# A two-layer hybrid encoder on one Trainium2 core: v's second projection with its weights split early, merge products placed behind two heads, delta output by token tile

## The chip, the cores and the metric

The kernel runs on one core of one Trainium2 chip. The metric is device time in microseconds (us) of one execution, and the time of a kernel is the median over its runs. A core has five engines: TensorE (PE in the profile; PEld is its weight load), VectorE (DVE), ScalarE (ACT), GpSimd (POOL) and SyncE (SP, which here only issues DMAs). Each runs its own instructions in order, and they wait for one another with semaphores. SP, ACT and POOL each have queues of DMAs.

## The reference

x is 256 tokens by 1024. Two layers follow, and a final RMSNorm. A layer computes:

```
h = rmsnorm(x, norm_w[l])
proj = h @ w_in[l]                       # 1024 x 10272
(q_a, k_a, v_a, ab_a, z_a, q_b, k_b, v_b, z_b, gate_a, gate_b) = split(proj)
y_a = gated_delta_branch(q_a, k_a, v_a, ab_a, z_a, ...)        # 8 heads of 128, both directions
y_b = diff_attention_branch(q_b, k_b, v_b, z_b, cos, sin, ...) # 8 heads, two softmax maps each
x = x + (sigmoid(gate_a) * (y_a @ w_pa[l]) + sigmoid(gate_b) * (y_b @ w_pb[l])) @ w_out[l]
```

The delta branch runs a short convolution of five taps and a silu over q, k and v, and then the gated delta rule in chunks, forward and backward, for which a unit lower triangular matrix per head and chunk has to be inverted. Its output is normalised per head and multiplied with silu(z). The attention branch subtracts lambda times a second softmax map from the first, applies the result to v_b, normalises and multiplies with silu(z). All is float32.

## The kernel before

**Products.** A float32 weight is split into a high part that TensorE can take in one pass (`hi`, fp32r, a cast on ScalarE, L229) and the rest (`lo`, a subtraction on VectorE, L231). The activations are split likewise, and each product is three products: high by high, high by low, low by high. `weights` (L207) loads 512 columns of a weight in four parts of 256 rows (512 KB each, L225), splits each, and hands out eight k-tiles. By default the loads use the tag `raw` with three buffers, the parts `hi` and `lo` with two each. `homes` lets a part lie in a big tile that is free at that time (`A`, `ktm`, `vtm`, `B`), and `spare` puts a raw load into the tag `w4a`. `later` queues a part's cast and subtraction behind given instructions of ScalarE and VectorE, `held` moves a load to ScalarE's DMA queue behind the first normalisation.

**Three ways to multiply.** `proj_tm` (L236) accumulates both token tiles (of 128 tokens) together, k-tile by k-tile, in two of the four banks with tag `p`. `proj_by_tile` (L257) does one token tile through all eight k-tiles and then the other, each product queued behind the one before it. `proj_fm` (L285) gives channels by tokens and serves the convolutions: 96 products of 256 columns per half, and `evac_conv` (L511) reads the banks with four multiply-adds of VectorE per block of 128 channels (L521).

**Order.** The kernel's instructions are put in order by a planner, which works by program order, given priorities (`tc.high_priority`), data, buffers and a simulated time. `tc.issue_after(ins)` (in the helper `behind`) queues an instruction behind another on its own engine and adds no wait between engines. What runs when on the chip is thus not what the program's text alone says.

**A layer.** First v's first projection by token tile (columns C_VB to C_VB + 511, L366), in layer 0 while the tokens are still being loaded and normalised: `prenorm` (L327) normalises a token tile, transposes it on TensorE and splits it (L195, L196). Then, in the text's order (L877 to L905): k's convolution in two halves, v's second projection (`vb_part(1)`, through `proj_tm`), the decays, q's convolution, the projections of the attention's q and k, the weighted Gram matrices, the blockwise inversion on VectorE (`substitute`), v's convolution. The projection of beta and decay (`abp`, L480) comes ahead of k's convolution; its weights `wab` and `wabr` use the tags `raw` and `hi`. Eight `head`s follow (L823): scores (`sc`, L833), exponentials (L842), transposes (`at`, L853), a copy (L855), value products (`av`, L859). The projections of z lie between them.

**Merges.** `merges(g)` (L691) joins inverted blocks of 32 into blocks of 64 and then of 128, for two groups of four heads. A generator, it is advanced by `step`: loads; the first products (`y64p`, L717, queued behind `mark["av"]`); the second products (`zt64` at L731 and `z64` at L737, 64 and 32 of size 32 by 32) queued behind `mark["at"]`, the last transpose of the latest head; then the same for 128 (L754, L762). In the text both groups' second products come behind head 6 and ahead of head 7, with everything up to the chunks (`chunks`, L769) at high priority:

```
head(6)
with tc.high_priority(offset=HP):
    step(mg)
    step(mg)
    step(mg)
    in_step(chunks(0), chunks(1))
head(7)
```

**Output.** The attention's output goes through `gated` (L934), its gate and its projection; beside them the chunks finish. For the delta output, 16 squared sums (L976) of both token tiles are followed by one factor on GpSimd for both (`rsqrt_rows`, 16 columns, L136 and L137), then `gated`: 16 multiplications on VectorE (L939) with `split_T` (transposes `pt_ya` at L189, splits at L198 and L199) per half and token tile, and the projection `pa`. Its gate `ga` (L948) is projected at the same time.

**The start.** Token tile 0's loads, v's first two parts, token tile 1's loads and the taps `cwr` go on SP's queue, part 2 on ScalarE's behind the first normalisation's squares, part 3 on SP's when a raw buffer is free.

## Time and profile before

| | |
|---|---|
| median of 3 runs | 791.64 us (789.83 to 792.08) |
| the profiled execution | 792.5 us, its span 790.7 us |
| TensorE busy, weight load busy | 761.9 us (96%), 652.2 us (82%) |
| VectorE busy | 557.9 us (71%) |
| ScalarE busy | 479.2 us (61%) |
| GpSimd busy | 99.9 us (13%) |
| mean granted TensorE clock | 0.990 |
| DMA | 126.92 MB, 161 GB/s over the span |

The span reaches from the first to the last instruction of the profiled execution; the execution's own time is 1.8 us longer. Products are pipelined and their ends modelled, so a busy TensorE is not one at its peak; but idle time between rows is idle. In a row of the timeline stand the start, the time until the last of the group ended, engine, line, operation, the tiles written and read, shapes and count, and in brackets the engine's idle time before it and what ended it; "issue" there means that the profile shows nothing it waited for. The granted clock is 1.00 or 0.50 in any stretch.

### The profile page before, as it was taken

To read this page: it belongs to the slowest core of one execution; us is meant where nothing else is said; L and a number is where in the kernel's file an instruction comes from. 1 tells how busy PE (TensorE), PEld (TensorE's weight loads), DVE (VectorE), ACT (ScalarE), POOL (GpSimd) and SP (SyncE) were. 2 spreads that over 40 slices of the span, in tenths; PEclk is the share of its full clock that TensorE was granted. 3 is DMA by queue.
4 is the path that set the end of the run, shared out by engine and by line. 5 is a ranking of instruction groups with operands and counts; after the bars stand their busy time and mean duration, and the time that the engine had idled before them with its cause. 6 is when DMAs were issued, how large, how long until landed. Compare 5 with 4: busy or idle time off the path is not lost.

```text
span 790.7 us, 13805 instructions
## 1 busy us (share of the span) xinstructions
PE 761.9 (96%) x5222; PEld 652.2 (82%) x5222; DVE 557.9 (71%) x1047; ACT 479.2 (61%) x1043; POOL 99.9 (13%) x133
## 2 busy tenths in 40 slices
PE   7989999999998999999999899999999899999996
PEld 4989889887787888878889788899778688887884
DVE  4587968999973653477656977989998445546772
ACT  4557776556676745664534778655577675446551
POOL 4200471100030100100000025510001110001000
PEclk9999999999999999999999999999999899999998
DMA  6555657564395534357625557655446925344631
GB/s 195 153 181 159 204 170 202 162 173 145 110 204 177 187 109 132 107 161 239 219 80 165 156 165 236 186 167 162 140 139 190 205 85 183 124 123 125 218 129 53
DMA packets 77746, 126.92 MB, mean 161 GB/s; under 512 B 19679, under 2 KB 20015, under 8 KB 77680
## 3 DMA queue, kind: packets, MB, share of 16 engines
q1 hardware_dynamic: 73182, 115.22, 48.7%
q0 software_dynamic: 3936, 9.77, 4.9%
q8 instruction: 41, 0.67, 0.4%
q10 hardware_dynamic: 562, 1.05, 0.4%
q14 instruction: 25, 0.20, 0.1%
HBM read 121.27 MB, written 4.75 MB: 159 GB/s over the span
## 4 chain that ended last, share of the span: by engine, by line
PE 80%; DVE 9%; ACT 4%; DMA 4%; issue 2%; POOL 0%; SPq 0%; POOLq 0%; ACTq 0%; DVEq 0%
PE pp_vb L280 3%; DMA raw_q<-in_w_in_dram 3%; PE pp_qk L244 2%; PE sc L833 2%; PE pp_qk L245 2%; PE pp_qk L243 2%; PE av L859 2%; PE pp_o L280 2%; PE pf_v L295 2%; PE pp_gb L243 2%; PE pp_za L244 2%; PE pf_v L299 2%; PE pf_v L297 2%; PE pp_gb L245 2%; PE pp_gb L244 2%
## 5 line engine op out<-in xcount | busy, mean ns | idle before, releaser
L244 PE MATMUL pp_qk<-lo_qk,hT 128*128 128x512 f32 x128 | 51.3, 401 | 1.0 <-DVE lo_qk L231 1.0
L245 PE MATMUL pp_qk<-hi_qk,hT 128*128 128x512 f32 x128 | 50.1, 391 | 0.0
L243 PE MATMUL pp_qk<-hi_qk,hT 128*128 128x512 f32 x128 | 46.1, 398 | 0.7 <-ACT hi_qk L229 0.7
L231 DVE TENSOR_TENSOR lo_qk<-raw_qk,hi_qk 128x1024 fp32r<-128x1024 f32 x32 | 40.2, 1256 | 9.0 <-ACT hi_qk L229 8.7
L229 ACT CAST hi_qk<-raw_qk 128x1024 fp32r<-128x1024 f32 x32 | 33.5, 1046 | 20.1 <-PE pp_qk L245 12.6
L231 DVE TENSOR_TENSOR lo_pb<-raw_pb,hi_pb 128x1024 fp32r<-128x1024 f32 x16 | 19.6, 1224 | 34.2 <-ACT hi_pb L229 34.2
L295 PE MATMUL pf_q<-hT,hi_q 128*128 128x256 f32 x128 | 36.3, 288 | 0.2 <-ACT hi_q L229 0.2
L295 PE MATMUL pf_v<-hT,hi_v 128*128 128x256 f32 x128 | 36.5, 289 | 0.0
L297 PE MATMUL pf_v<-hT,hi_v 128*128 128x256 f32 x128 | 36.2, 285 | 0.0
L297 PE MATMUL pf_q<-hT,hi_q 128*128 128x256 f32 x128 | 35.8, 284 | 0.0
L295 PE MATMUL pf_k<-hT,hi_k 128*128 128x256 f32 x128 | 35.7, 283 | 0.0
L297 PE MATMUL pf_k<-hT,hi_k 128*128 128x256 f32 x128 | 35.6, 283 | 0.0
L842 ACT ACTIVATE es<-sc,mx 128x256 f32<-128x256 f32 x64 | 29.7, 472 | 9.6 <-DVE mx L840 9.5
L299 PE MATMUL pf_q<-hT,lo_q 128*128 128x256 f32 x128 | 35.2, 290 | 0.0
L231 DVE TENSOR_TENSOR lo_gb<-raw_gb,hi_gb 128x1024 fp32r<-128x1024 f32 x16 | 19.6, 1222 | 21.9 <-ACT hi_gb L229 21.9
L299 PE MATMUL pf_v<-hT,lo_v 128*128 128x256 f32 x128 | 34.6, 285 | 0.0
L299 PE MATMUL pf_k<-hT,lo_k 128*128 128x256 f32 x128 | 34.3, 286 | 0.0
L231 DVE TENSOR_TENSOR lo_k<-raw_k,hi_k 128x1024 fp32r<-128x1024 f32 x16 | 19.6, 1223 | 16.2 <-ACT hi_k L229 16.2
L521 DVE SCALAR_TENSOR_TENSOR cvk<-pf_k,cw,cvk 128x254 f32<-128x254 f32 (+1 forms) x64 | 29.3, 478 | 2.0 <-ACT cvk L517 1.2
L521 DVE SCALAR_TENSOR_TENSOR cvv<-pf_v,cw,cvv 128x254 f32<-128x254 f32 (+1 forms) x64 | 29.7, 475 | 0.6 <-ACT cvv L517 0.5
L521 DVE SCALAR_TENSOR_TENSOR cvq<-pf_q,cw,cvq 128x254 f32<-128x254 f32 (+1 forms) x64 | 29.6, 475 | 0.7
L231 DVE TENSOR_TENSOR lo_ga<-raw_ga,hi_ga 128x1024 fp32r<-128x1024 f32 x16 | 19.4, 1223 | 15.0 <-ACT hi_ga L229 15.0
(361 smaller groups left out, 2508.3 us busy)
## 6 DMA issues: line engine op xcount, KB each, us to landing
raw_qk<-in_w_in_dram SPq DMA_DIRECT2D x32, 512.0 KB, 3.7
raw_k<-in_w_in_dram SPq DMA_DIRECT2D x16, 512.0 KB, 3.7
raw_q<-in_w_in_dram SPq DMA_DIRECT2D x16, 512.0 KB, 3.7
raw_v<-in_w_in_dram SPq DMA_DIRECT2D x16, 512.0 KB, 3.8
raw_zb<-in_w_in_dram SPq DMA_DIRECT2D x16, 512.0 KB, 3.6
raw_za<-in_w_in_dram SPq DMA_DIRECT2D x16, 512.0 KB, 3.7
raw_gb<-in_w_in_dram SPq DMA_DIRECT2D x16, 512.0 KB, 4.3
raw_o<-in_w_out_dram SPq DMA_DIRECT2D x16, 512.0 KB, 4.5
```

What stands on the lines that cost most here:

```text
L229: high = S.copy(hi[:, :, :n], raw[:, :, :n]).ins
L231: mark[nm, kp] = high, V.tensor_tensor(lo[:, :, :n], raw[:, :, :n], hi[:, :, :n].bitcast(F32), ALU.subtract).ins
L243: T.matmul(o, act[kt // 4][:, 0, kt % 4, ts_], hi, start=kt == 0, stop=False)
L244: T.matmul(o, act[kt // 4][:, 0, kt % 4, ts_], lo, start=False, stop=False)
L245: mark["proj"] = T.matmul(o, act[kt // 4][:, 1, kt % 4, ts_], hi, start=False, stop=kt == KT - 1).ins
L280: mark["proj"] = T.matmul(o, a_, w_, start=kt == 0 and a_ is ah and w_ is hi, stop=kt == KT - 1 and a_ is al).ins
L295: T.matmul(o, hi[:, cs], act[kt // 4][:, 0, kt % 4, :], start=first, stop=False, skip_group_check=True)
L297: T.matmul(o, hi[:, cs], act[kt // 4][:, 1, kt % 4, :], start=False, stop=False, skip_group_check=True)
L299: T.matmul(o, lo[:, cs], act[kt // 4][:, 0, kt % 4, :], start=False, stop=done, skip_group_check=True)
L521: V.scalar_tensor_tensor(ca[:, o0:o1], acc[:, b, o0 + sft : o1 + sft], cw[:, j, cb : cb + 1], ca[:, o0:o1], ALU.mult, ALU.add)
L833: mm = T.matmul(sp[n][:, qt * SEQ : (qt + 1) * SEQ], qkT[h // 4][rows, 0, h % 4, qt * P : (qt + 1) * P], qkT[h // 4][rows, 1, h % 4, :], s ...
L842: S.activation(es[:, n, qt, :], spv[:, qt, :], AF.Exp, bias=mx[:, n, qt : qt + 1], accum_out=s_all[:, h, n, qt : qt + 1])
```

## The change

- *v's second projection* goes by token tile through `proj_by_tile` instead of `proj_tm`. Its four parts get homes of their own: a pair with tag `p8`, the second half of the tile `B` (now twice as long) and `vtm`. Its raw loads use `w4a`. Parts 0 and 1 are split behind the split of token tile 1's second half, parts 2 and 3 behind the second and third part of k's first half. In layer 0 the loads of parts 0 and 1 go on ScalarE's queue, behind that split.
- *Loads one by one*, in layer 0's start: part 1 of v's first projection on ScalarE's queue behind token tile 0's first squares, token tile 1's loads behind its second squares, part 2 behind the cast of part 0; `wab` behind the cast of part 2.
- *Smaller moves*: `wab` and `wabr` use the tags `w2a` and `w2c`; sine and cosine are one activation; the lambda sums (`lp`, `lq`, `ls`, `neglam`) move behind the gates of beta and decay.
- *Merges*: group 0's second products stay behind head 6, group 1's come behind head 7, each queued behind that head's last value product and no longer behind its last transpose.
- *Delta output*: squares, factor and `gated` for token tile 0, and then for token tile 1.

```
-                with behind(mark["norm", 0][0] if kp in held else None):
-                    (nc.scalar if kp in held else nc.sync).dma_start(
+                load = (held or {}).get(kp)
+                with behind(load):
+                    (nc.scalar if load else nc.sync).dma_start(
...
-    def tokens(m):
+    def tokens(m, load=None):
         for i in range(2):
-            nc.sync.dma_start(out=xt[i][:, m, :], in_=xdr[:, i, m, :])
+            with behind(load):
+                (nc.scalar if load else nc.sync).dma_start(out=xt[i][:, m, :], in_=xdr[:, i, m, :])
...
-        places = list(homes((("A", 1), ("ktm", 1), ("vtm", 1), ("B", 1)), f"vb{l}"))
-        later, between = {}, None
+        places = list(homes((("A", 1), ("ktm", 1), ("vtm", 1), ("B", 2)), f"vb{l}"))
+
+        places2 = pair(f"wvb{l}")
+        places2 = [t_.rearrange("p x b t -> p x (b t)").rearrange("p x (k c) -> p x k c", k=2)
+                   for t_ in places2] + [places.pop(), *homes((("vtm", 1),), f"vb{l}1")]
+        later, between, held = {}, None, {}
         if l == 0:
             later[0] = None, mark["norm", 0][1]
             def between(kt):
                 if kt == 2:
+                    held[1] = mark["square", 0, 0]
                     later[1] = mark["split", 0, 0]
                 elif kt == 4:
-                    tokens(1)
+                    tokens(1, mark["square", 0, 1])
+                    held[2] = mark["vb00", 0][0]
...
-        wab = wpool.tile([P, 2, 512], F32, tag="raw", name=f"wab{l}", bufs=3)
...
+        wab = work.tile([P, KT, 32], F32, tag="w2a", name=f"wab{l}", bufs=2)
+        with behind(None if l else mark["vb00", 2][0]):
+            (nc.sync if l else nc.scalar).dma_start(
+                out=wab, in_=wl[:, C_AB : C_AB + 32].rearrange("(k p) c -> p k c", p=P))
+        wabr = work.tile([P, KT, 64], F32R, tag="w2c", name=f"wabr{l}", bufs=3)
...
-            first = mark["at"]
+            first = mark["av"]
...
         conv("k", C_KA, 0, 0)
         conv("k", C_KA, 0, 1)
-        vb_part(1)
+        for _ in proj_by_tile(hT, wl, C_VB + 512, evac_v(1), f"vb{l}1", places2, spare=range(4),
+                              later={0: mark["split", 1, 1], 1: mark["split", 1, 1],
+                                     2: mark[f"k{l}0", 1], 3: mark[f"k{l}0", 2]},
+                              held={} if l else dict.fromkeys(range(2), mark["split", 1, 1][0])):
+            pass
         log_decays()
...
         head(6)
         with tc.high_priority(offset=HP):
-            step(mg)
+            step(mg[:1])
+        head(7)
+        with tc.high_priority(offset=HP):
+            step(mg[1:])
             step(mg)
             step(mg)
             in_step(chunks(0), chunks(1))
-        head(7)
...
-        def gated(o_, z_, r_, nw_, yT, nm):
+        def gated(o_, z_, r_, nw_, yT, nm, tiles=range(NM)):
             for i in range(2):
-                for m in range(NM):
+                for m in tiles:
...
+        ro = small.tile([P, NM, NH], F32, tag="ro", name=f"ro{l}")
+        yaT = pair(f"yaT{l}")
         for m in range(NM):
             for h in range(NH):
                 S.activation(sqj[:, :P], osb(h // 4, m)[:, h % 4, :], AF.Square,
                              accum_out=sso[:, m, h : h + 1])
-        V.tensor_tensor(sso, sso, rq2, ALU.mult)
-        ro = small.tile([P, NM, NH], F32, tag="ro", name=f"ro{l}")
-        rsqrt_rows(ro.rearrange("p c h -> p (c h)"), sso.rearrange("p c h -> p (c h)"), 1.0 / P, 16)
-        V.scalar_tensor_tensor(ro, ro, 0.5, rq, ALU.mult, ALU.mult)
-        yaT = pair(f"yaT{l}")
-        gated(osb, za, ro, nw[:, 0:1], yaT, f"ya{l}")
+            V.tensor_tensor(sso[:, m], sso[:, m], rq2[:, m], ALU.mult)
+            rsqrt_rows(ro[:, m], sso[:, m], 1.0 / P, NH)
+            V.scalar_tensor_tensor(ro[:, m], ro[:, m], 0.5, rq[:, m], ALU.mult, ALU.mult)
+            gated(osb, za, ro, nw[:, 0:1], yaT, f"ya{l}", (m,))
         branch(yaT, w_pa[l], gta, f"pa{l}")
```

54 lines of the change are left out of this document (23 added, 31 removed).

## The prediction

> **What bounds the kernel now.** I read the page first, then the list of what TensorE waited for, then busy time by stage, then single stretches of the timeline.
>
> ```profile
> span 790.7 us, 13805 instructions
> PE 761.9 (96%) x5222; PEld 652.2 (82%) x5222; DVE 557.9 (71%) x1047; ACT 479.2 (61%) x1043; POOL 99.9 (13%) x133
> ...
> PE pp_vb L243 <- DVE cvk L521: 3.1, 2, 1.5
> PE pp_ga L244 <- DVE lo_ga L231: 2.1, 2, 1.0
> PE pp_vb L244 <- DVE lo_vb L231: 1.0, 2, 0.5
> ```
>
> TensorE is the bound: it stands idle for 790.7 - 761.9 = 28.8 us in all, and no edit of this change takes a matrix product away. So a gain can only be idle time of TensorE, or time in which its clock was granted at half. The three waits shown each come twice, once per layer; the first and the third are v's second projection, the second is the gate beside the delta output. The next view gives TensorE's busy time in four stretches (columns: the stretch, its length, busy time and count of PE, PEld, DVE, ACT, POOL, then the granted clock, the DMA share and GB/s).
>
> ```profile
> 28.40:50.50 22.10, 22.10 (x184) 21.89 (x183) 13.97 (x24) 13.18 (x19) 0.00 (x0) 1.00 0.53 150
> 50.50:75.00 24.50, 22.35 (x139) 19.34 (x138) 20.36 (x37) 18.39 (x49) 0.00 (x0) 1.00 0.52 153
> 435.00:460.00 25.00, 22.88 (x143) 19.86 (x143) 21.24 (x37) 17.93 (x48) 0.00 (x0) 1.00 0.54 163
> 331.00:350.00 19.00, 17.95 (x87) 14.63 (x86) 12.68 (x28) 10.27 (x19) 3.11 (x2) 1.00 0.47 144
> ```
>
> Idle is length less PE busy: 2.15 and 2.12 us around v's second projection, 1.05 us at the delta output of layer 0 (that of layer 1 has the other half of the wait for lo_ga), none in k's convolution ahead of the projection. The fourth place is the merge, once per layer, in the same columns:
>
> ```profile
> 242.86:246.27 3.41, 1.38 (x24) 0.89 (x17) 1.83 (x2) 3.31 (x9) 0.00 (x0) 1.00 0.62 187
> 246.27:249.68 3.41, 3.41 (x50) 2.54 (x53) 1.44 (x6) 2.41 (x10) 0.00 (x0) 0.50 0.81 297
> 625.15:628.56 3.41, 0.95 (x37) 0.68 (x36) 1.23 (x1) 1.54 (x3) 0.00 (x0) 1.00 0.31 114
> 628.56:631.97 3.41, 3.24 (x72) 2.40 (x71) 0.00 (x0) 2.24 (x6) 0.00 (x0) 0.50 0.91 300
> 631.97:635.39 3.42, 3.42 (x96) 3.14 (x96) 2.02 (x6) 2.51 (x11) 0.00 (x0) 0.50 0.03 13
> ```
>
> A stretch in which TensorE is busy for 1.38 (or 0.95) of 3.41 us is followed by one (or two) at half the clock. The idle time is 2.03 and 2.46 us here; the half clock costs half of 3.41 us in layer 0 and half of 3.24 + 3.42 us in layer 1, so 1.7 and 3.3 us. All that the merge could give is 2.03 + 2.46 + 1.7 + 3.3 = 9.5 us.
>
> **v's second projection.** Rows of the timeline (start, length) show the largest wait and the spare time ahead of it, and one of the chain what 24 products of this form take:
>
> ```profile
> 58.24 0.47 PE L243 MATMUL pp_vb<-hi_vb,hT 128*128 128x512 f32 x1 [1.54 <-DVE cvk L521]
> ...
> 38.10 1.05 ACT L229 CAST hi_k<-raw_k 128x1024 fp32r<-128x1024 f32 x1 [1.83 <-PE pf_k L297]
> ...
> 39.18 1.23 DVE L231 TENSOR_TENSOR lo_k<-raw_k,hi_k 128x1024 fp32r<-128x1024 f32 x1 [1.66 <-ACT hi_k L229]
> ...
> 386.78 5.45 PE pp_o L280 x24
> ```
>
> The 1.54 us are a bank: this product is the first into the accumulator of the other token tile, and VectorE had not read k's first convolution out of it. Four lo parts of v, 4 x 1.23 = 4.9 us, stand on VectorE among those reads. The change makes them earlier, in buffers that the convolution's weights don't use, and runs all 24 products of token tile 0 before the first of tile 1. Like the 24 of the row from the output projection they take 5.45 us in the first bank, longer than the 1.54 us wait, and VectorE comes sooner as well. Both waits go: 2.15 + 2.12 = 4.27 us. What it adds ahead: four times 1.05 us of ScalarE and 1.23 us of VectorE per layer, beside k's weights. These have gaps of 1.83 and 1.66 us per pair of k-tiles, each of which holds one part; the cover is thin, and where it fails a k product waits up to 1.05 or 1.23 us. I take 4.0 (ends 4.3 and 0). What is late next is VectorE, 20.36 of 24.50 us busy in that stage, but it loses 4.9 us there.
>
> In layer 0 two of the four loads are issued by ScalarE's queue behind the splits of token tile 1, two instructions; what is queued behind them there is k's first cast, not needed before the convolution. The weights of beta and decay leave the convolution's raw and hi buffers, and lambda's sums move behind them; sine and cosine become one activation. All of this lies off TensorE's waits: nothing.
>
> **The start.** Part 0 of v's weights comes late, and part 3 shows what a load takes by itself:
>
> ```profile
> 1.71 8.09 DMA raw_vb<-in_w_in_dram
> ...
> 11.40 7.76 PE pp_vb L280 x19
> ...
> 12.15 0.40 SPq L225 DMA_DIRECT2D raw_vb<-in_w_in_dram  x1
> ...
> 15.63 1.04 ACT L229 CAST wB_vb<-raw_vb 128x1024 fp32r<-128x1024 f32 x1 [0.18 <-DMA raw_vb<-in_w_in_dram]
> ```
>
> 8.1 us against 15.63 - 12.15 = 3.5. With the loads one by one, part 0 could land up to 4.6 us sooner. But the loads that are held back stand behind part 0 on SP's queue already, so it need not gain from their going; and part 2 is now issued only when part 0 has been cast (after 9.8 at today's landing, and 3.5 us later it is there, at 13.3, where tile 1's normalisation waits for its lo part). I take nothing, with ends of 2 us gained (less than half of the 4.6, as tile 1 needs the later loads too) and 1.5 us lost (part 0 sharing with the loads that now come from another queue).
>
> **The merge.** TensorE's rows, layer 1 first, with ScalarE's copy of head 6's weights, and then the like of layer 0:
>
> ```profile
> 623.28 1.33 PE L717 MATMUL y64p<-T,A 32*32 32x32 f32 x128
> ...
> 625.64 0.45 PE L731 MATMUL zt<-U__96,y 32*32 32x32 f32 x32
> 628.73 0.49 PE L731 MATMUL zt<-U__96,y 32*32 32x32 f32 x21 [2.64 <-issue]
> ...
> 630.02 2.08 PE L833 MATMUL sc<-qkT 64*128 64x256 f32 x8
> ...
> 626.27 0.58 ACT L855 COPY aT<-at 128x512 f32<-128x512 f32 x1
> ...
> q8 instruction: 1, 0.02, 3.0%
> ...
> 246.21 0.98 PE L833 MATMUL sc<-qkT 64*128 64x256 f32 x2 [2.03 <-issue]
> ...
> 241.88 0.72 PE L731 MATMUL zt<-U__96,y 32*32 32x32 f32 x62
> ...
> 243.41 0.58 ACT L855 COPY aT<-at 128x512 f32<-128x512 f32 x1
> ...
> 249.12 0.94 PE L731 MATMUL zt<-U__96,y 32*32 32x32 f32 x64
> ...
> 251.91 0.76 ACT L747 ACTIVATE T<-z 32x256 f32<-32x256 f32 x2
> ...
> 255.03 2.08 PE L754 MATMUL y128p<-T,A 64*64 64x64 f32 x64
> 257.04 1.16 PE L859 MATMUL av<-vb,aT 128*128 128x128 f32 x8
> ```
>
> In layer 1 TensorE stops for 2.64 us in the middle of a run of equal products that wait for nothing. The row of queue 8 is from DMA traffic at 626 to 628 us: one block of instructions was fetched there, during the stop. I read the stop as TensorE having run out of instructions, since 128 + 96 small products (each with a weight load) go by in about 3 us. The change lets 8 score products and head 6's 8 value products go first. Layer 1: scores follow at 625.64 and take half of 2.08, to 626.7; the copy is done at 626.85; the value products take about 1 us, to 627.9; of the 32 products that were left before the stop, 16 remain, 0.2 us; if the block comes at 628.73 as before, the stop is 0.6 + 0.15 in place of 2.64, a gain of 1.9. The stretch 625.15 to 628.56 is then busy for about 2.6 us and not 0.95, so the clock should hold: 3.3 more. After the second products TensorE may run dry until head 7's exponentials free their banks, about 1 us: 4.0 taken. Layer 0: scores from 241.88 to 242.9, copy done at 243.99, value products to 244.9, second products to 246, block at 246.21: about 1.2 us idle for 2.03, a gain of 0.8; the stretch is busy for about 2.2 of 3.41 us, and whether that holds the clock I count at half of 1.7, less 0.6 dry: 1.0. Together 5.0 (ends 9.5 gained and 2 lost, the latter if the stop and the half clock stay and 1 us of dry time comes in each layer).
>
> **Delta output.** VectorE runs all 16 products of the gated output in a row, ahead of a weight part:
>
> ```profile
> 337.93 4.29 DVE L939 SCALAR_TENSOR_TENSOR kq<-kq,ro,za 128x128 f32<-128x128 f32 x16
> ...
> 343.41 0.50 PE L244 MATMUL pp_ga<-lo_ga,hT 128*128 128x512 f32 x1 [1.05 <-DVE lo_ga L231]
> ...
> 334.07 2.90 POOL L137 TENSOR_TENSOR ro<-rspre,mhalf 128x16 f32<-128x16 f32 x1
> ...
> 344.41 1.40 DVE L199 SCALAR_TENSOR_TENSOR yaT<-pt_ya,nw,yaT 128x512 fp32r<-128x512 f32 x2
> ...
> 348.54 1.03 PE L189 MATMUL pt_ya<-ident,kq 128*128 128x128 f32 x8
> ```
>
> By token tile they come in two runs of 8, 2.15 us each, and GpSimd's power of 2.90 us becomes two of about half. One weight part can slip between, which is worth 1.05 us per layer. Added are one multiply, one GpSimd pair and one scaling per layer, small and beside other work. I take 1.4 of 2.10 (ends 2.1 gained, 1 lost if both runs fall ahead of a weight part).
>
> **Sum.** 4.0 + 0 + 5.0 + 1.4 = 10.4. The profiled execution took 792.5 us (span 790.7, 1.8 around it), so 782.1; the median of the runs is 791.64, 0.86 below it, so 781.2.
>
> **Rivals.** *The stop follows the products*: what counts is that small products come in a burst, wherever it stands, so the idle time and half clock stay or move to group 1's burst. For it: the "issue" rows don't say what was missing. Against: the stop is in the middle of one burst. The merge gives nothing and 5.4 is left of the sum, 786.2. [...] Chance 0.15.
>
> *The clock stays at half*: what holds the clock is not busy time as the view counts it, and small products and scores on half the rows don't count. For it: the stretch 628.56 to 631.97 was busy for 3.24 us and one more at 0.50 followed. Against: 242.86 to 246.27 and 625.15 to 628.56 are the idlest of the stage, and both times the half clock came right behind. The merge then gives idle time alone, 1.9 + 0.8 less the dry 1.6, so 1.1, and the median is 791.64 - 6.5 = 785.1. [...] Chance 0.15.
>
> *Early parts collide*: the gaps of 1.83 and 1.66 us are missed and each part costs k's convolution 0.5 us, 2 x 4 x 0.5 = 4.0 us, v's whole gain: 785.2. For it: the gaps are only 0.8 and 0.4 us longer than a part. Against: ScalarE and VectorE are busy for 13 and 14 of 22.1 us there. Chance 0.08.
>
> *The delta chain ends late*, which ends slower: group 1's second products ran at 249.12, head 7's value products at 257.04 + 1.16. If these keep their place, group 1 starts 9.1 us later. Its next step ran at 255.03, 2.4 us after its last input (251.91 + 0.76), so the chain of merges and chunks is 6.7 us late. The chain's last transposes ran at 348.54, 2.7 us after the banks were read (344.41 + 1.40): that is the slack. 4.0 us per layer are left, and where the chain sets the end the idle time saved beside it is no gain: 8.0 - 4.0 of v = 4.0 lost, 795.6. It decides if head 7's value products come over 2.4 + 2.7 us after 249.12. Against: scores of head 7 go first now, and without the stop its exponentials come sooner. Chance 0.08.
>
> *More than I take*: clock held in both layers and the start 2 us sooner, 10.4 + 2 + 2.5 = 14.9: 776.7. Chance 0.12. *The forecast*: 0.42, from 778 to 785.
>
> **Numbers.** 781.2 us. The range goes from 775.5 to 789.5: it holds the forecast, the three rivals that take one term away and most of the case with more, and leaves out the late chain and the ends of all unknowns together. This kernel's measurement tells 0.3% from no change, 2.4 us: faster is below 789.3. Forecast, the three one-term rivals and the case with more give 0.92 if each stood alone; of that I count 0.1 for two terms failing together, 0.09 of it within 0.3% and 0.01 slower, which joins the late chain's 0.08. Faster 0.82, same 0.09, slower 0.09.
>
> **What would show it.** Right: no wait of pp_vb for cvk or lo_vb, and TensorE busy throughout 50 to 65; no "issue" stop above 1 us at zt and no half-clock stretch in layer 1; L939 in runs of 8 and no wait of pp_ga for lo_ga; first product of v within 1.5 us of 11.4. Wrong: pf_k waiting for hi_k or lo_k in k's convolution; a stop of 2 us in front of group 1's products; pp_pa waiting for yaT.

## The result and the profile after

| | before | after |
|---|---|---|
| median | 791.86 us (789.83 to 795.11, 4 runs) | 781.91 us (780.45 to 784.95, 4 runs) |
| the profiled execution | 792.5 us, span 790.7 us | 782.13 us, span 780.3 us |

The ratio is 0.9888, 95% interval 0.9856 to 0.992: about 10 us less, and the prediction said 781.2. The total came out nearly as worked out. Its terms did not, and most of what follows is about that.

First the head of the page of the changed kernel.

```profile
span 780.3 us, 13801 instructions
...
PE 758.2 (97%) x5222; PEld 651.5 (83%) x5222; DVE 557.0 (71%) x1051; ACT 474.9 (61%) x1042; POOL 101.0 (13%) x137
```

The count of products is the same, and TensorE's idle time is 780.3 - 758.2 = 22.1 us where it was 28.8. That is 6.7 us of the 10.4 by which the span is shorter; the rest is busy time that became shorter, through the clock above all (mean granted 0.994 after 0.990; 0.004 of 780 us are 3.1 of the 3.7). Next, three lines of the list of what TensorE waited for (total, times, longest).

```profile
PE abq L480 <- ACT abT L477: 2.8, 1, 2.8
...
PE zt L735 <- issue: 1.1, 1, 1.1
...
PE pf_k L296 <- ACT vb L348: 1.0, 1, 1.0
```

The three waits that the prediction quoted (pp_vb for cvk, pp_ga for lo_ga, pp_vb for lo_vb) are gone. In their place stand two waits for ScalarE, each once and both early in layer 0, and what is left of the stop among the merge's small products. Busy time in the stages that were shown of before (columns as there):

```profile
28.00:50.50 22.50, 19.68 (x139) 19.41 (x138) 13.12 (x27) 13.23 (x19) 0.00 (x0) 0.85 0.48 140
50.50:72.00 21.50, 21.50 (x139) 19.39 (x138) 17.54 (x37) 11.83 (x35) 0.00 (x0) 1.00 0.36 108
...
432.00:455.00 23.00, 23.00 (x151) 20.90 (x151) 16.88 (x33) 13.92 (x45) 0.00 (x0) 1.00 0.30 87
...
325.00:346.50 21.50, 21.50 (x126) 18.74 (x125) 13.57 (x30) 13.19 (x42) 3.67 (x4) 1.00 0.38 120
```

In v's second projection of both layers (second and third row) and at the delta output (fourth) TensorE now has no idle time at all. The first row is new trouble: 22.50 - 19.68 = 2.8 us idle in k's convolution of layer 0, at a mean clock of 0.85, where before it was busy throughout at 1.00.

How far each stage moved is read from where the same work begins. Rows of TensorE, of the kernel before and then of the changed one: the first product of v in layer 1, and the first product of q's convolution, which follows v's second projection, in both layers (v's first product in layer 0 was at 11.40 before).

```profile
67.54 0.36 PE L295 MATMUL pf_q<-hT,hi_q 128*128 128x256 f32 x1
...
398.33 0.71 PE L280 MATMUL pp_vb<-wA_vb,hT 128*128 128x512 f32 x2
...
451.56 0.36 PE L295 MATMUL pf_q<-hT,hi_q 128*128 128x256 f32 x1
```

```profile
9.03 3.45 PE L281 MATMUL pp_vb<-wA_vb,hT 128*128 128x512 f32 x6
...
69.00 0.28 PE L296 MATMUL pf_q<-hT,hi_q 128*128 128x256 f32 x1
...
395.80 1.55 PE L281 MATMUL pp_vb<-wA_vb,hT 128*128 128x512 f32 x4
...
445.87 0.28 PE L296 MATMUL pf_q<-hT,hi_q 128*128 128x256 f32 x1
```

From v's first product to q's convolution layer 1 took 53.23 us and takes 50.07: 3.2 gained. Layer 0 took 56.14 and takes 59.97: 3.8 lost. The start is 2.4 us earlier, and at 69.00 all of it is gone, with 1.5 more. Why is seen in ScalarE's rows of the changed kernel:

```profile
24.69 1.05 ACT L230 CAST wvb<-raw_vb 128x1024 fp32r<-128x1024 f32 x1 [3.92 <-DMA raw_vb<-in_w_in_dram]
28.54 1.05 ACT L230 CAST wvb<-raw_vb 128x1024 fp32r<-128x1024 f32 x1 [2.80 <-DMA raw_vb<-in_w_in_dram]
...
33.26 0.35 ACT L477 COPY abT<-abp 64x256 f32<-64x256 f32 x1
```

These are the early parts 0 and 1. Their loads were issued at 17.39 and 18.49 us and landed at 24.7 and 28.5, after 7.3 and 10.0 us; v's part 3 of the kernel before took 3.5. ScalarE stands at both casts, for 3.92 and 2.80 us, and runs nothing else in that time. Behind them come a copy of v, two table loads (1.28 us each) and the copy `abT`, for which TensorE waits:

```profile
33.66 1.06 PE L480 MATMUL abq<-id,abT 64*128 64x32 f32 x4 [2.82 <-ACT abT L477]
```

```profile
20.00:28.00 8.00, 7.29 (x41) 6.28 (x42) 4.24 (x12) 1.82 (x4) 1.34 (x3) 1.00 0.99 325
28.00:33.52 5.52, 2.84 (x24) 2.63 (x22) 2.15 (x7) 4.71 (x8) 0.00 (x0) 1.00 0.67 191
33.52:40.35 6.83, 6.69 (x30) 6.63 (x31) 4.45 (x11) 3.70 (x5) 0.00 (x0) 0.50 0.33 100
```

The second fence gives busy time again. In its second row TensorE is idle for 2.7 of 5.52 us, and then 6.83 us at half the clock. These hold 30 products, the next 6.83 us, at the full clock, hold 58, most of them of the same form; so the half clock is put at half of 6.69, another 3.3, here and likewise below. Layer 0's own waits in v's second projection are gone all the same (2.15 us before, none now); what it lost, it lost ahead of them.

The merge of layer 1, TensorE's rows and the stretch around the stop:

```profile
622.42 0.32 PE L735 MATMUL zt<-U__96,y 32*32 32x32 f32 x15
623.86 0.59 PE L735 MATMUL zt<-U__96,y 32*32 32x32 f32 x47 [1.11 <-issue]
```

```profile
620.62:624.03 3.41, 2.18 (x49) 1.54 (x49) 2.59 (x4) 2.00 (x8) 0.00 (x0) 1.00 0.37 74
624.03:627.44 3.41, 2.83 (x91) 2.39 (x82) 1.14 (x4) 3.30 (x14) 0.00 (x0) 1.00 0.78 288
```

The stop is 1.11 us and no longer 2.64, after 15 products (before: after 32), and the clock stays at 1.00. In layer 0 there is no stop there. But group 1's products of layer 0 are late:

```profile
241.32 1.33 PE L721 MATMUL y64p<-T,A 32*32 32x32 f32 x128
...
257.27 1.05 PE L863 MATMUL av<-vb,aT 128*128 128x128 f32 x8
258.26 0.72 PE L735 MATMUL zt<-U__96,y 32*32 32x32 f32 x62
...
261.91 2.08 PE L758 MATMUL y128p<-T,A 64*64 64x64 f32 x64
```

They ran at 249.12 before, and the next step at 255.03. Measured from the merge's first products (239.52 before, 241.32 after) that step comes 15.5 us later before and 20.6 after: the delta chain is 5.1 us late. And the delta output, on VectorE:

```profile
336.09 2.18 DVE L949 SCALAR_TENSOR_TENSOR kq<-kq,ro,za 128x128 f32<-128x128 f32 x8
...
343.47 2.18 DVE L949 SCALAR_TENSOR_TENSOR kq<-kq,ro,za 128x128 f32<-128x128 f32 x8
```

Two runs of 8, with the weight parts between them.

### The profile page after: what moved, and what is told of

Its sections match the earlier page's. It is cut to its first block, busy times and chain, and to the rows that moved or that the text cites. A ratio compares the mean times of both kernels' runs of the same rounds, so it can differ in the third digit from the quotient of the medians.

```text
span 780.3 us, 13801 instructions
## 1 busy us (share of the span) xinstructions
PE 758.2 (97%) x5222; PEld 651.5 (83%) x5222; DVE 557.0 (71%) x1051; ACT 474.9 (61%) x1042; POOL 101.0 (13%) x137
## 4 chain that ended last, share of the span: by engine, by line
PE 81%; DVE 7%; DMA 6%; ACT 4%; issue 1%; POOL 0%; SPq 0%; POOLq 0%; ACTq 0%; DVEq 0%
PE pp_vb L281 4%; DMA raw_q<-in_w_in_dram 3%; DMA raw_vb<-in_w_in_dram 3%; PE pp_qk L245 2%; PE pp_qk L246 2%; PE pp_qk L244 2%; PE pp_o L281 2%; PE pf_v L296 2%; PE pf_k L300 2%; PE pf_k L296 2%; PE pf_k L298 2%; PE pp_za L245 2%; PE pf_v L300 2%; PE pf_v L298 2%; PE pp_za L246 2%; PE pp_gb L245 2%
## 5 line engine op out<-in xcount | busy, mean ns | idle before, releaser
L296 PE MATMUL pf_k<-hT,hi_k 128*128 128x256 f32 x128 | 37.0, 294 | 1.0 <-ACT vb L348 1.0
L298 PE MATMUL pf_k<-hT,hi_k 128*128 128x256 f32 x128 | 36.8, 292 | 0.0
L230 ACT CAST hi_pb<-raw_pb 128x1024 fp32r<-128x1024 f32 x16 | 16.8, 1049 | 23.9 <-PE pp_pb L246 23.1
```

Of the source, the lines that this page charges most:

```text
L230: high = S.copy(hi[:, :, :n], raw[:, :, :n]).ins
L296: T.matmul(o, hi[:, cs], act[kt // 4][:, 0, kt % 4, :], start=first, stop=False, skip_group_check=True)
L298: T.matmul(o, hi[:, cs], act[kt // 4][:, 1, kt % 4, :], start=False, stop=False, skip_group_check=True)
```

## The experiments

The theory after the result: the whole is a sum of parts that went otherwise than worked out. Layer 0's v lost by ScalarE's waits for loads what layer 1's gained; the merge's new place made the delta chain late; and the output by token tile was worth far more than 1.4 us because it took that late chain off the end. The rival is the prediction's own account: four parts, each worth its term.

**Each part undone alone**, four kernels on one chip, beside the kernel before at 790.49 us (18 runs).

v's second projection as before, in the changed kernel:

```
-        for _ in proj_by_tile(hT, wl, C_VB + 512, evac_v(1), f"vb{l}1", places2, spare=range(4),
...
+        proj_tm(hT, wl, C_VB + 512, 512, evac_v(1), f"vb{l}1")
```

> The changed kernel with v's second projection as before (both token tiles together, weights through the shared buffers, loads on SP). Theory from the two traces: in layer 1 the new way gained 3.2 us (first product of q's convolution 5.7 us earlier than before where it had been 2.5 earlier), in layer 0 it lost about 3.9 (2.4 us gained at the first product, 1.5 us lost at q's convolution), because ScalarE waits in its order for the loads of parts 0 and 1. Undoing it then changes the total by -3.9 + 3.2, so about 781.2, with TensorE's wait of 2.8 us ahead of abq gone and the waits of pp_vb for cvk and lo_vb back in both layers. Rival, the prediction's own term: the new way is worth 4.0, so 785.9.

Measured: 783.34 us, ratio 0.9908 (0.9889 to 0.9927). The wait for the bank is back, the wait at `abq` and the half clock behind it are gone:

```profile
PE pp_vb L244 <- DVE cvk L523: 3.1, 2, 1.5
```

By the medians the new projection is worth about 1.5 us net over both layers, between the theory's 781.2 and the rival's 785.9; the intervals of the two ratios leave open anything from a small loss to a little over 4 us. What the profiles show is a gain in one layer and a loss in the other, as the theory says: from v's first product to q's convolution layer 1 takes 53.4 us again (50.07 in the changed kernel), and layer 0 takes 57.5 (59.97).

The merge as before (both groups behind head 6, queued behind its last transpose):

```
-            first = mark["av"]
+            first = mark["at"]
...
-            step(mg[:1])
-        head(7)
-        with tc.high_priority(offset=HP):
-            step(mg[1:])
+            step(mg)
...
+        head(7)
```

> The changed kernel with both groups' second products behind head 6 and its last transpose, as before. From the start of the first merge products to the start of the branch projection the changed kernel is 4.3 us faster in layer 0 and 4.9 in layer 1, merge and delta output together. Theory: the merge is most of it, 7 to 9 us over both layers, so 789 to 791, with stops of over 2 us marked issue and half clock back in both layers. Rival, the prediction's sizes: 5.0, so 786.9. If the token tiles of the delta output carried it: under 3, so below 785.

Measured: 786.11 us, ratio 0.9945 (0.9925 to 0.9965). TensorE's row and the stretch behind it, in layer 1:

```profile
624.54 0.49 PE L735 MATMUL zt<-U__96,y 32*32 32x32 f32 x21 [2.65 <-issue]
```

```profile
624.30:631.12 6.82, 6.58 (x154) 5.37 (x155) 1.46 (x3) 4.40 (x15) 0.00 (x0) 0.50 0.50 157
```

Stop and half clock are back with the old place: 2.65 us and half of 6.58. In layer 0 a stop of 1.2 us is back, but no half clock, which the theory had in both layers; the time, too, is the rival's 786.9 rather than the theory's 789 to 791.

The delta output for both token tiles at once:

```
-            V.tensor_tensor(sso[:, m], sso[:, m], rq2[:, m], ALU.mult)
-            rsqrt_rows(ro[:, m], sso[:, m], 1.0 / P, NH)
-            V.scalar_tensor_tensor(ro[:, m], ro[:, m], 0.5, rq[:, m], ALU.mult, ALU.mult)
-            gated(osb, za, ro, nw[:, 0:1], yaT, f"ya{l}", (m,))
+        V.tensor_tensor(sso, sso, rq2, ALU.mult)
+        rsqrt_rows(ro.rearrange("p c h -> p (c h)"), sso.rearrange("p c h -> p (c h)"), 1.0 / P, 16)
+        V.scalar_tensor_tensor(ro, ro, 0.5, rq, ALU.mult, ALU.mult)
+        gated(osb, za, ro, nw[:, 0:1], yaT, f"ya{l}")
```

> The changed kernel with the delta output's squares, factor and products for both token tiles at once, as before. The prediction's size: 1.4 us, 783.3, and the wait of pp_ga for lo_ga of about 1 us back per layer. Rival: the chain of chunks ends later in the changed kernel (in layer 0 its first products start 5.7 us later against the first merge products), and the token tiles are what keeps that off the end; then 3 to 6 us, 785 to 788, with pp_pa waiting for yaT.

Measured: 791.43 us, ratio 1.0009 (0.9992 to 1.0026). Without this part the whole change is worth nothing that can be measured. The list of waits, and busy time around the wait in layer 0:

```profile
PE pp_pa L244 <- ACT yaT L198: 5.0, 2, 2.5
```

```profile
347.23:350.64 3.41, 1.75 (x9) 1.04 (x9) 3.41 (x4) 1.82 (x3) 0.00 (x0) 1.00 0.58 178
350.64:354.05 3.41, 3.41 (x10) 2.73 (x9) 0.91 (x2) 0.69 (x1) 0.00 (x0) 0.50 0.75 247
```

The delta's projection waits 2.5 us in each layer for the transposed output, with VectorE busy throughout the stretch shown, and a stretch of 3.41 us at half clock follows in each. The wait of pp_ga for lo_ga, on which the size of 1.4 us rested, is not back. This is the rival "the delta chain ends late", with the sign that the prediction put on the whole change: "pp_pa waiting for yaT".

The first loads as before (part 1, token tile 1 and part 2 not held back):

```
-                    held[1] = mark["square", 0, 0]
...
-                    tokens(1, mark["square", 0, 1])
-                    held[2] = mark["vb00", 0][0]
+                    tokens(1)
+                    held[2] = mark["norm", 0][0]
```

> The changed kernel with the first loads as before: parts 0 and 1 and the second tokens together on SP, part 2 on ScalarE behind the first normalisation. If loads one by one brought the first product from 11.4 to 9.0 us: it goes back to 11 to 11.5. The end: theory that everything after follows the first product: 2.4 us, 784.3. Rival: in layer 0 the late landing of v's early parts sets when k's convolution runs, so the end moves by less than 1 us. Third: the first part's earlier landing was chance of the small load on GpSimd's queue, and the first product stays at 9 to 9.5.

Measured: 783.73 us, ratio 0.9914 (0.9896 to 0.9932), about 2 us more than the changed kernel. v's first product:

```profile
9.92 3.45 PE L281 MATMUL pp_vb<-wA_vb,hT 128*128 128x512 f32 x6 [1.03 <-ACT hT L195]
```

0.9 us later than 9.03, and 1.5 earlier than the 11.40 of before, with the first loads in the order of before. The kernel before with useless products added (below), whose start is not edited at all, has its first product at 9.39, among the 9.03 to 9.65 of the eleven profiles with the loads one by one. So the 11.40 belongs to that one execution, and no gain of the start is shown: the 1.8 us by which this median is longer are not clear of nothing by the intervals either.

**Two parts undone together.** The four undone singly cost 1.4 + 4.2 + 9.5 + 1.8 us (against the 781.91 of the changed kernel), 16.9 together, more than the change is worth. So they aren't separate. The next kernel has both the merge and the delta output as before; v and the start stay changed.

> The changed kernel with both the merge's second products (both groups behind head 6) and the delta output (both tiles at once) as before; what stays of the change is v's second projection and the loads one by one. Undone one by one, the merge cost 4.2 us and the delta output 9.5. Theory (the two act together: the split of the groups makes the delta chain end later, and only the output by token tile keeps that off the end): undone together they cost what the stages from the merge to the delta output differ by in the profiles, 9.2 us, so 789.5 to 791, no better than before within its scatter. Rival (each part is worth what its undoing cost): 4.2 + 9.5 = 13.7, so 794 to 796, clearly slower than before.

Measured: 790.03 us beside 791.58 of before, ratio 0.9985 (0.9962 to 1.0008). The theory's band is 789.5 to 791; separate parts would have given 794 to 796 and are out. With the ratios, each to the kernel before on its own chip, times 791 us, the change takes apart as follows:

| what is changed | ratio to before | us gained |
|---|---|---|
| v and start | 0.9985 | 1.2 |
| v, start, merge | 1.0009 | -0.7 |
| v, start, delta output | 0.9945 | 4.4 |
| all | 0.9888 | 8.9 |

The merge alone loses 1.9 us, the delta output alone gains 3.2, and the two together gain 7.7, so 6.4 us come from the pair. The intervals of the ratios are 0.0017 to 0.0032 to either side, 1.3 to 2.5 us; taken together, in squares, they leave the 6.4 clear of zero and the 1.9 not.

**Is it the split of the groups or the place?** The change of the merge has two edits: group 1 goes behind head 7, and each group goes behind value products and no longer behind transposes. One kernel keeps the second edit and undoes the first:

```
-            step(mg[:1])
-        head(7)
-        with tc.high_priority(offset=HP):
-            step(mg[1:])
+            step(mg)
             step(mg)
             step(mg)
             in_step(chunks(0), chunks(1))
+        head(7)
```

> The changed kernel with one thing of the merge undone: both groups' second products stand behind head 6, as before, but still behind head 6's value products and not between its transposes and these. It differs from the kernel with the merge as before, which took 786.11 us, only in this place. Theory (the place behind the value products carries the merge's gain, the split between heads 6 and 7 nothing): 780.5 to 783, as the changed kernel, a stop of at most 1.1 us after some 15 small products in layer 1 and no half clock there. Rival (the split carries it): 785 to 787 with the stop of 2.6 us after some 32 small products in layer 1 again.

Measured: 781.29 us beside 790.81, ratio 0.9863 (0.9833 to 0.9893). TensorE's row in layer 1:

```profile
623.07 1.04 PE L735 MATMUL zt<-U__96,y 32*32 32x32 f32 x62
```

No stop at all in this execution and no half clock. The place behind the value products carries the gain; the split between the heads adds nothing that can be measured. Whether the place would also pay with the delta output as before, no run shows. Over all profiles the old place behind the transposes had a half-clock stretch in layer 1's merge in 4 of 4, the new one in 1 of 10.

**What is the stop?** The kernel before with products that nobody needs, 64 calls per layer, into an unused part of a bank:

```
+            if h == 0:
+                for _ in range(64):
+                    T.matmul(op_[0:32, SEQ : SEQ + 32], aT[0:32, 0, 0:32], aT[0:32, 0, 0:32],
+                             start=True, stop=True)
```

> The kernel before, with 64 more products of 32 x 32 (two TensorE instructions each) into an unused part of a bank behind head 0's values in each layer: work without a use, which moves every later TensorE instruction of layer 0 by 128 places and of layer 1 by 256. Theory (the stop among the small products is TensorE waiting for its next block of instructions, fetched every 256): layer 0's stop moves by about 64 of the small products against the kernel before, while layer 1's stays after the same count of them. Rival (the stop belongs to the group's own dependence, at the first products behind group 0's casts): both stops stay where they were in the order of work. Time: 4 to 12 us more than before, for 128 small products and what they push.

Measured: 809.41 us, one run, 19 us more than the runs beside it. The count in the expectation was wrong: the page has 5478 products where there were 5222, so each of the 64 calls came as two products, each with a weight load. Layer 0 was thus moved by 256 instructions and layer 1 by 512, whole steps in both, and with these numbers the theory, like the rival, leaves both stops at the same work: the run can't tell the two apart. The cost was more than the products' own 5 us per layer (an estimate: 128 at the 92 in 3.42 us of the first row below): behind them the clock went to half for 6.83 us in each layer. In layer 0:

```profile
191.16:194.58 3.42, 3.42 (x92) 3.09 (x92) 3.42 (x9) 1.74 (x8) 0.00 (x0) 1.00 0.52 143
194.58:201.40 6.82, 6.82 (x57) 5.79 (x54) 5.38 (x15) 1.18 (x5) 0.00 (x0) 0.50 0.07 25
```

TensorE was busy throughout both stretches, most of the first with the added products. TensorE's rows, layer 0's merge and then layer 1's:

```profile
253.62 0.59 PE L833 MATMUL sc<-qkT 64*128 64x256 f32 x2 [0.17 <-issue]
...
640.10 0.47 PE L731 MATMUL zt<-U__96,y 32*32 32x32 f32 x33
643.01 0.35 PE L731 MATMUL zt<-U__96,y 32*32 32x32 f32 x20 [2.44 <-issue]
...
648.71 0.39 PE L731 MATMUL zt<-U__96,y 32*32 32x32 f32 x13 [2.06 <-issue]
```

Layer 1 stops after 33 of the small products as it did after 32, and a second time 5.7 us later. Layer 0's stop is at the same scores, but only 0.17 us of 2.03 are left. What tells theory and rival apart is a count in the traces: the instructions of TensorE's queue (products, weight loads and a few semaphore instructions), numbered from 0 in order of time. In the kernel before, the first instruction behind the stop is number 3265 in layer 0 and 8385 in layer 1, which is 20 x 256 further on. Here the three are 3521, 8897 and 9153. In the 14 profiles there are 22 stops marked "issue" and longer than 0.15 us among the merges' products and the scores behind them; each ends at such a number, 193 above a multiple of 256, whatever work stands there. In the changed kernel 8385 is the 16th small product and not the 33rd. So the stop keeps its place in the stream of instructions, in steps of 256, and not in the work. The kernel before has 41 fetches on queue 8 for 10536 such instructions, one for every 257. Those that belong to its two stops begin at 243.87 and 626.34, 2.3 and 2.4 us ahead of the end of the stop, and here, in layer 0, at 251.4, 2.2 us ahead of it. The stops are 2.03 and 2.64 us long there and 0.17 us here; that work at hand covers the difference is a reading that no run shows. Why the fetch began sooner against the work here, no run shows.

**Layer 0's loads.** The changed kernel once more, and two versions of it on the same chip.

> The changed kernel once more, nothing edited, so that the next kernels stand beside it on one chip. The theory of layer 0's beginning (ScalarE, which takes its instructions in order, stands at the casts of the early weight parts 0 and 1 until their loads have landed, 3.92 + 2.80 us, and the copies behind them reach TensorE late) expects the wait at the transposes of the gates' columns again, 1.6 to 2.9 us. How much a half clock adds behind it, 0 or about 3.4 us, is left open, because one of the earlier kernels with the same order of work up to there had the wait without the half clock. Time: 781 to 783.

Measured: 781.44 us beside 790.42, ratio 0.9886 (0.985 to 0.9922); six runs, 778.39, 780.01, 780.18 and then 782.70 to 782.84. The profiled one is the 778.39. ScalarE's rows:

```profile
24.53 1.05 ACT L230 CAST wvb<-raw_vb 128x1024 fp32r<-128x1024 f32 x1 [2.83 <-DMA raw_vb<-in_w_in_dram]
26.45 1.06 ACT L230 CAST wvb<-raw_vb 128x1024 fp32r<-128x1024 f32 x1 [0.86 <-DMA raw_vb<-in_w_in_dram]
```

The second load landed 2.1 us sooner than in the first profile, the wait at `abq` is 0.6 us, less than the 1.6 expected at least, and the clock holds there. The same kernel thus has this cost in one execution and hardly in another. Of the seven profiles of kernels that load and cast the early parts as the change does, five show the wait at 2.4 us or more with half a clock behind it. The next version casts layer 0's parts later, part 0 behind the second part of k's first half, part 1 behind the third, parts 2 and 3 behind the fourth:

```
-                                     2: mark[f"k{l}0", 1], 3: mark[f"k{l}0", 2]},
+                                     2: mark[f"k{l}0", 1], 3: mark[f"k{l}0", 2]} if l else
+                                    {0: mark["k00", 1], 1: mark["k00", 2], 2: mark["k00", 3], 3: mark["k00", 3]},
```

> Layer 0's four weight parts of v's second projection are cast later: part 1 with k's second convolution step, part 2 with the third, part 3 with the fourth, instead of two of them early in v's first projection; layer 1 stays. Theory (ScalarE's wait for loads): the wait of 3.92 + 2.80 us at the casts goes from in front of the copies of v, so the 2.8 us wait at the gates' transposes falls below 1 us and the half-clock stretch of 6.83 us at 33.5 us is gone; 2.8 to 5 us less than the changed kernel beside it, 777 to 779. Rival (that part of the layer is set by the small loads on GpSimd's queue and by k's loads, whoever stands in front): the wait only changes its name, k's convolution waits for its high and low halves, and the time is within 0.3% of the changed kernel.

Measured: 779.11 us, ratio 0.986 (0.9827 to 0.9894). A wait for a load remains on ScalarE ahead of the copies, but at one cast and not at two:

```profile
25.64 1.05 ACT L230 CAST wvb<-raw_vb 128x1024 fp32r<-128x1024 f32 x1 [2.76 <-DMA raw_vb<-in_w_in_dram]
```

TensorE's wait at `abq` is 1.2 us, above the expected 1, and no stretch at half clock follows. The time is 2.3 us below the changed kernel's, less than the 2.8 expected at least and at the edge of the rival's 0.3%. Then the same with the loads on SyncE's queue (`held={}` in both layers):

> As the kernel before it in this list, and layer 0's loads of those parts are issued on SyncE's queue and not on ScalarE's. Theory (ScalarE's wait for loads): the casts are already late enough, so the queue makes no difference beyond 1 us; 776 to 779. Rival (the loads themselves collide): with the parts behind k's five loads on SyncE's queue these land sooner, k's convolution starts earlier, and this is the faster of the two by 1 to 2 us; against it, on SyncE's queue the parts could land too late for their casts, and v's second products wait for the casts as in the kernel before, about 3 us, 779 to 781.

Measured: 777.85 us, ratio 0.9842 (0.981 to 0.9874), six runs from 777.22 to 779.57. The first two of these loads did not go behind k's, as the expectation has it: the planner put them right behind part 0 of v's first projection. A row of SyncE's queue (two of its three loads are these), and busy time in two of the stretches that the changed kernel was shown in:

```profile
2.74 8.02 SPq L226 DMA_DIRECT2D raw_vb<-in_w_in_dram  x3
```

```profile
28.00:33.52 5.52, 5.52 (x43) 5.14 (x42) 1.86 (x11) 2.53 (x6) 0.00 (x0) 1.00 0.41 135
33.52:40.35 6.83, 6.83 (x59) 6.83 (x59) 5.56 (x10) 5.62 (x8) 0.00 (x0) 1.00 0.55 166
```

TensorE is busy throughout both, at the full clock, and ScalarE waits at none of the casts of the early parts 0 and 1. It waits sooner: part 1 of v's first projection, whose load on ScalarE's queue (issued at 3.91) now runs beside theirs, is cast at 12.04, after a wait of 2.45 us, where it was 9.48 in the version above. Against the changed kernel on the same chip the time is 3.6 us less by the medians, though the intervals of the two ratios overlap. A second measurement on another chip:

> The version with layer 0's parts cast late and loaded on SyncE's queue once more, beside the kernel before and the one above on one chip: 777 to 780. In its six runs so far none was over 779.6, where the changed kernel beside it had three of six over 782.7. If ScalarE's wait for the loads was what sometimes cost those 3 to 4 us, again no run lies over 780.5.

Measured: 777.46 us beside 791.58, ratio 0.9822 (0.9795 to 0.9848), six runs from 776.59 to 779.8, none over 780.5. The profiled one is the slowest, 779.8, and shows what the earlier loads can cost: TensorE waits for part 1 of v's first projection (1.1 us for its cast and 0.8 for its lo part), and half the clock follows, half of 6.32 us or 3.2 lost.

```profile
12.01:15.43 3.42, 1.57 (x6) 0.86 (x5) 1.83 (x2) 2.77 (x6) 0.26 (x1) 1.00 0.79 290
15.43:22.25 6.82, 6.32 (x19) 4.35 (x17) 5.49 (x9) 3.93 (x5) 6.73 (x8) 0.50 0.78 184
```

By the ratios of both measurements this version is about 4 us faster than the changed kernel. Whether the later cast or the earlier load does it isn't settled: the first alone gave 2.3 us, with an interval that takes in all of it.

**Both groups behind head 6 in that version**, behind its value products:

> The version with layer 0's early weight parts cast late and loaded on SyncE's queue, and with both groups' second products behind head 6, in front of head 7, but behind head 6's value products and not in front of them. Theory (in the changed kernel the split pays by what stands between the two groups' small products: with 128 products in a row a stop or a half clock comes in layer 1, and the split has only 64 in a row): 3 to 5 us more than the version that it is made from, 781 to 783. Rival (the split itself costs, because the delta chain starts 5.7 us later behind it, and the place behind the value products is what counts): 2 to 5 us less, 773 to 776.

Measured: 778.01 us, ratio 0.9828 (0.9802 to 0.9853), the same as its neighbour's 777.46. Both expectations were wrong: the split is worth neither 3 to 5 us nor costs 2 to 5. It was this result that led to the kernel on the place alone, above.

## Why the prediction was right and where it was wrong

**What bounds the kernel.** Right: no product went, and the gain is idle time and half clock of TensorE.

**v's second projection.** The mechanism held: both waits went, TensorE is busy throughout the stage in both layers, and layer 1 gained 3.2 us where 2.1 was counted on for it. The step that failed is the sentence on layer 0's loads: "what is queued behind them there is k's first cast, not needed before the convolution. [...] All of this lies off TensorE's waits: nothing." It looked at the two instructions that issue the loads and not at the casts that wait for them. Those stood on ScalarE for 3.92 and 2.80 us, ahead of copies for which TensorE waits. The rival "early parts collide" had the collision in k's convolution with a cover of 0.8 and 0.4 us; the place was the loads. Net, v and the start gave 1.2 us, give or take 1.8, and not 4.0.

**The start.** Taken as nothing, with 2 us as its upper end; undoing it costs 1.8 us, which the intervals don't hold clear of nothing, and the first product's 2.4 us lie between executions (9.39 with the start of before). So no run shows that taking nothing was wrong.

**The merge.** The working for layer 1 held step by step: 15 small products ahead of the stop (16 said), 1.11 us of stop (0.75 said), a stretch busy for 2.18 of 3.41 us (2.6 said), clock held, 0.58 us dry behind it (about 1 said). In another execution of the same kernel the clock did not hold (below). Undone, it costs 4.2 us; 5.0 was the term. Wrong was the choice that the split does not make the chain late. The prediction's own condition, head 7's value products over 5.1 us after 249.12, was met: 257.27, 8.15 later, and still 6.35 if the 1.80 us by which the merge as a whole began later are taken off. Head 7's value products simply kept their place, 257.04 before, as the rival supposed. Its arguments against ("scores of head 7 go first now, and without the stop its exponentials come sooner") left out that a whole head and products of the attention's gate now stand between the two groups. Taken by itself the merge gave, in place of 5.0, nothing or a loss (-1.9).

**Delta output.** The mis-sized term. 1.4 was taken, 2.1 at most: the wait for lo_ga. Alone it gave 3.2, with the late chain behind the merge 7.7 more than v and the start. What was not seen is that the same edit shortens the end of the very chain that the merge makes late: token tile 0's factor is there at 335.42 and its 8 multiplications are done well before token tile 1's factor at 342.73, where with both at once the factor came at 340.43 and all 16 multiplications behind it. Without the edit pp_pa waits 5.0 us for yaT, two stretches of 3.41 us at half clock follow, 3.4 more, and 1.5 us are smaller waits that the changed kernel doesn't have (1.1 for lo_pa, 0.4 at the transposes): 9.9, against 9.5 measured. The wait for lo_ga, which was the whole of the term, is not among them; it is there, 2.0 us in all, only with the merge as before as well.

**The sum.** 10.4 predicted, 8.9 by the ratios, 10.0 by the medians. That it came so near is luck: v's missing 2.8 and the merge's missing 6.9 were made up by 8.2 that the delta output gave beyond its term (1.8 alone, 6.4 in the pair). The late-chain rival treated its mechanism as a case apart, with a chance of 0.08; it occurred, and another part of the same change was its remedy. Without that remedy its price was nearly the 4.0 us per layer that were worked out: 2.5 of wait and 1.7 of half clock.

**The rivals on clock and stop.** Neither came true in the changed kernel's profile. The stop keeps to steps of 256 instructions (its end is at 3265 and 8385 in the kernel before, at 8385 in the changed one), and the 41 fetches for 10536 instructions agree with the step.

On the clock two rows of neighbouring size stand side by side. That of the changed kernel's first profile is above: 2.18 of 3.41 us busy, the next stretch at 1.00 (laid on the grid of 3.413 us on which the clock changes in the two profiles of before and after: short of the end of the span the records at half are 1 or 2 such steps long, 3.41 and 6.83 us, and those at full clock 6 to 216, 20.48 to 737.28 us). Those of its second profile, and two from layer 1 of the kernel with v's second projection as before:

```profile
616.71:620.12 3.41, 2.13 (x103) 1.79 (x102) 2.17 (x7) 2.40 (x10) 0.00 (x0) 1.00 0.54 156
620.12:623.53 3.41, 2.99 (x9) 2.52 (x10) 0.67 (x2) 3.29 (x11) 0.00 (x0) 0.50 0.57 204
...
434.65:438.06 3.41, 1.74 (x8) 1.25 (x8) 3.19 (x9) 1.88 (x11) 0.00 (x0) 1.00 0.65 187
438.06:441.47 3.41, 3.41 (x18) 2.84 (x18) 3.06 (x7) 2.85 (x6) 0.00 (x0) 1.00 0.00 2
```

Here 2.13 of 3.41 us busy cost the clock, 2.18 did not, and 1.74 did not either. Over all 14 profiles, each laid on its grid from where its record of the clock begins, and for windows at full clock, the clock fell behind every one that was busy for at most 1.56 us; between 1.70 and 2.13 it fell 5 times and held 15 times; from 2.18 on it held, but for the added products above, where TensorE was busy throughout. So busy time as the view counts it does not decide alone, as the rival on the clock had it; what does is open.

## What to carry to other kernels

Parts of a change that touch one chain are priced together: first what each does to the chain's end, then what is left for TensorE to wait for. When a load moves to another queue, follow not only the instruction that issues it but the first one that needs it, and read what stands behind that on its engine (ScalarE ran nothing else for 3.92 and 2.80 us here); and look at which load of the old order it now runs beside. A short stop of TensorE may cost as much again in clock (2.46 us idle and 3.3 of half clock in layer 1's merge of the kernel before), so a stop is worth breaking up with work that is ready anyway, and the place in the order of work does that where a split between stages need not.

## What was not expected of the hardware

A load of 512 KB took 7.3 and 10.0 us from issue to landing at 17 to 28 us of the changed kernel, where the 16 DMA engines were busy for 0.99 of the time from 20 to 28 us, against 3.5 us for v's part 3 in the kernel before, at a share of 0.65; and the second of the two was there 2.1 us sooner in another execution of the same kernel. The first of these executions had 6.83 us at half clock behind the wait and took 782.13 us, the other had none there and took 778.39, though it lost 3.41 us to half the clock in layer 1's merge. So a load's landing may move the time of the kernel by more than the wait for it; which of the other runs lost clock where isn't known.
